# A hybrid encoder layer: an eleventh tile in the long convolution's ring, its room from shared gate rows and from two norm weights folded into the output matrix

## The chip, the cores and the metric

The kernel runs on one core of a Trainium2 chip. The core's engines work side by side, each through its own list of instructions: TensorE (PE) multiplies matrices into the banks of PSUM, VectorE (DVE), ScalarE (ACT) and GpSimd (POOL) do the elementwise work, and SyncE (SP) does nothing but issue transfers between the device memory (DRAM) and the on-chip memory (SBUF, 128 partitions). Transfers are carried by 16 DMA engines. The metric is the device time of one execution in microseconds (us), as a median over several runs.

## What is computed

One layer of a bidirectional encoder over 2048 positions of width 1024, in float32. A projection feeds two mixers: a Hyena group (512 channels), whose long convolutions are done through Fourier transforms, and an mLSTM group (4 heads of 128). Each mixer's output is normalised by groups with a weight per channel, the two are put side by side, and one output matrix follows; then cross-attention to 256 memory rows, and a feed-forward block. The part that matters:

```python
def _group_rms_norm(x, g, n_groups):
    xg = x.reshape(*lead, n_groups, c // n_groups)
    xg = xg * rsqrt(mean(xg * xg, axis=-1, keepdims=True) + EPS)
    return xg.reshape(*lead, c) * g

for o, gate in enumerate((g1, g2)):                       # Hyena
    conv = irfft(rfft(z, n=2 * L) * spec[:, o], n=2 * L)[:, :L]
    z = gate * (conv + z * skip[o])

y_hy = _group_rms_norm(_hyena(...), hy_norm_g, 8)         # 8 groups of 64
y_ml = _group_rms_norm(_mlstm_bidirectional(...), ml_norm_g, 4)
mixed = concatenate([y_hy, y_ml], axis=-1)
h = h + mixed @ w_out
h = h + cross_attention(rms_norm(h), rms_norm(mem), wq, wk, wv, wo)
h = h + square(relu(rms_norm(h) @ ff_w1)) @ ff_w2
out = rms_norm(h)
```

## The kernel before

**Matrix products.** Most products are done in three passes on operands split into a high and a low part (L355, L358, L359). `split` makes the two parts with one copy on ScalarE and one subtraction on VectorE (L366); `split_gain` does the same with a factor per row (L372 and L373). Weights come through SBUF tiles `wn` of 128x512 (the first block of the attention through `we`), loaded by SP and then split into `wh` and `wl`.

**Order of work.** The layer runs as several generators whose steps are woven together, so that PE has work of one stage while another waits. The Hyena stage runs from about 350 us to about 1090 us beside the input projection. The projection of the memory rows for the attention (`memproj`) runs beside the last inverse transform, and the mLSTM scan and the attention come behind it. The instructions of a woven program are then ordered by the framework's scheduler, from its own estimates of when each can start. Each engine runs its list in order. A transfer is issued by an engine's queue, again in order: SP issues nearly all loads, POOL most of the stores, ACT a few. [...]

**The Hyena stage** (the function `hyena`) works on tiles of 128x1024 floats (512 KB), all from one ring with the tag `a`: `ta()` takes the next place in turn, and whoever takes it waits until all readers and writers of the tile that had the place before are done. The ring has ten places. The function's steps:

- Forward transform, 8 steps `j2`: `load1` loads a tile of `hy`, `spectrum` multiplies it (L173 and L186, the two lines of `beside`, which puts eight small products side by side on PE) and stores the result with a transfer of POOL.
- Frequency loop, 16 steps `i` for each of the two orders `o`: `load_filter` loads a block of the filter two steps ahead (`dm` and `fs`, L920), `load2` loads a block of the signal's spectrum one step ahead (`em`, L949, and `zs`), `response` makes the tiles `hr` and `hi`, then comes the complex product on VectorE, ScalarE and POOL, and `back` (L987 to L989) multiplies back and stores `gs` to `zg` with POOL. A step takes five ring places.
- Inverse transform, 8 steps `j2` for each `o`: `load3` loads two tiles of `zg` (L339) and one `gate` tile (L974), one step ahead; `beside` multiplies; VectorE multiplies by the gate (L1051). For `o` = 0 the next spectrum follows. For `o` = 1 the group norm follows, which takes a fourth place: POOL squares (L1060), VectorE sums, `bank_rsqrt` makes the reciprocal root in a PSUM bank, VectorE multiplies by it (L1064), POOL multiplies by the norm weight `ghy` (L1066, two products of 128x512) and issues four stores to `yh` (L1068).

The norm weights `ghy` and `gml` are vectors of 512 numbers, loaded into all 128 partitions by `bcast` (L377, on ACT's queue).

**memproj** multiplies on PE at L708 (keys' and values' weights `wm` with the memory rows `mt`), L725 (with `wq_t`) and L737 (with `wo`); its weights are loaded at L415, a few items ahead.

**The mLSTM scan** multiplies and scans chunk by chunk; for two chunks of 128 rows at a time it normalises: 64 instructions in all at L1356 multiply a head's 128x128 by its reciprocal root, which lies in a PSUM bank, and by `gml`. The bank is one of four that PE's products also use (L1322).

**The attention** takes blocks of 256 columns of `w_out` (16 of them, four for each of four column groups of the sequence), one block ahead, through `columns`.

Of the kernel before, what the change touches and what calls it, by code (L numbers as in the profile page):

```python
# [10 lines left out]
F32 = mybir.dt.float32  # L11
# [3 lines left out]
ALU = mybir.AluOpType  # L15
# [6 lines left out]
CH = 512  # L22
# [78 lines left out]
def packed(given):  # L101
    f32 = np.float32
    par = np.zeros((128, 192), f32)

    def put(at, v):
        v = np.asarray(v, f32).reshape(-1, 128).T
        par[:, at:at + v.shape[1]] = v

    for i, n in enumerate(("norm_mix_g", "norm_mem_g", "norm_x_g", "norm_ff_g")):
        put(8 * i, given[n])  # L110
    for i in range(3):
        put(32 + 20 * i, given["hy_conv_w"][0, i])
        put(44 + 20 * i, given["ml_conv_w"][0, i])
    put(92, given["hy_conv_b"])
    put(104, given["ml_conv_b"])
    par[:, 112:128] = given["ml_gate_b"]
    fw = np.zeros((128, 1280), f32)
    w3 = given["hy_filt_w3"][0].reshape(64, 2, 2, CH)
    for h in range(2):
        own = slice(64 * h, 64 * h + 64)  # L120
        for i, n in enumerate(("b1", "freq1", "b2", "freq2")):
            par[own, 128 + i] = given["hy_filt_" + n][0]
        fw[33 * h:33 * h + 33, own] = given["hy_filt_w1"][0]
        fw[own, 128 + 64 * h:192 + 64 * h] = given["hy_filt_w2"][0]
        fw[own, 256:] = w3[:, :, h].reshape(64, 2 * CH)
    return {"par": par, "fw": fw}


class Prog:
    def __init__(self, ctx, tc, a):  # L130
# [27 lines left out]
        self.cb, self.gb = par[:, 92:112], par[:, 112:128]  # L158
# [46 lines left out]
    def bank_rsqrt(self, pool, ss, n):  # L205
        nc, c = self.nc, ss.shape[1]
        m, ys = (pool.tile([128, c], F32, tag="br" + x, name="br" + x, bufs=2) for x in "my")
# [218 lines left out]
    def inproj_open(self, es):  # L426
# [22 lines left out]
        self.rx, self.rm = small[:, 340:356], small[:, 356:358]  # L449
# [455 lines left out]
    def hyena(self, es):  # L905
# [19 lines left out]
        def ta():  # L925
            return sb.tile([128, 2, CH], F32, tag="a", name="a", bufs=10)
# [5 lines left out]
        e2 = sb.tile([128, 64], F32, name="e2")[:, 0:32]  # L932
        nc.sync.dma_start(out=e2, in_=a["c_e2"])
        ghy = self.bcast(sb, a["hy_norm_g"], CH, "ghy")
# [78 lines left out]
        for o in range(2):  # L1013
# [27 lines left out]
            for j2 in range(8):  # L1041
# [19 lines left out]
                ms = sb.tile([128, 16], F32, tag="ms", name="ms", bufs=2)  # L1061
                nc.vector.tensor_reduce(ms, sqv, AX.X, ALU.add)
                rv = self.bank_rsqrt(sb, ms, 64)
                nc.vector.tensor_tensor(sqv, y, rv.unsqueeze(2).broadcast_to([128, 16, 64]), ALU.mult)  # L1064
                for jj in range(2):
                    nc.gpsimd.tensor_tensor(sq[:, jj], sq[:, jj], ghy, ALU.mult)  # L1066
# [9 lines left out]
    def gates(self):  # L1076
# [4 lines left out]
        with tc.tile_pool(name="m_g", bufs=1) as sg:  # L1081
            gts = sg.tile([128, 16, 16], F32, name="gts")
            nc.sync.dma_start(out=gts, in_=gt.rearrange("(n p) g -> p n g", p=128))
            arr = [sg.tile([128, 2, 16, 4], F32, name=f"arr{i}") for i in range(2)]
# [72 lines left out]
            negM = sg.tile([128, 128], F32, name="negM")  # L1157
            inter = sg.tile([128, 128], F32, name="inter")
# [68 lines left out]
    def mlstm(self, es):  # L1227
# [12 lines left out]
        gml = self.bcast(sb, a["ml_norm_g"], CH, "gml")  # L1240
# [58 lines left out]
        for n in range(16):  # L1299
# [51 lines left out]
            if n % 2:  # L1351
                rv = self.bank_rsqrt(sb, ss, 128)
                for i, y in enumerate(ys):
                    t0 = 128 * (n - 1 + i)
                    for h in range(4):
                        nc.vector.scalar_tensor_tensor(y[:, h], y[:, h], rv[:, 4 * i + h:4 * i + h + 1],  # L1356
                                                       gml[:, 128 * h:128 * h + 128], ALU.mult, ALU.mult)
# [41 lines left out]
    def columns(self, w, stage=None):  # L1399
# [4 lines left out]
        for k0 in range(0, 8 // (3 - n), n):  # L1404
            nat = (stage or self.stage)().rearrange("p (k c) -> p k c", k=n)
            self.nc.sync.dma_start(out=nat, in_=w[:, k0:k0 + n])
            self.split(hi[:, k0:k0 + n], lo[:, k0:k0 + n], nat)
# [31 lines left out]
    def attention(self, es):  # L1439
# [10 lines left out]
        for c in range(4):  # L1450
            items += [a["w_out"][0][:, 256 * i:256 * i + 256].rearrange("(k p) c -> p k c", p=128) for i in range(4)]
            items += [gd[h][:, 4 * k:4 * k + 4] for h in range(2) for k in range(2)] + [vw[i] for i in range(4)]

        def stream():
            nxt = self.columns(items.pop(0), lambda: A.tile([128, 512], F32, tag="e", name="we", bufs=4))
            for w in items:
                cur, nxt = nxt, self.columns(w)
# [750 lines left out]
```

## Time and profile before

| | before |
|---|---|
| median of 3 runs (lowest, highest) | 3053.21 us (3049.87, 3053.69) |
| the profiled execution | 3050.45 us |
| its span, first to last instruction | 3048.7 us |
| busy: PE, DVE, ACT, POOL | 97%, 64%, 49%, 41% |
| mean granted clock of PE | 0.992 |
| moved by DMA | 607 MB, 199 GB/s over the span |

The profile records one execution. A row of the waits reads: engine and line, what it waited for and the line that made that, then microseconds in total, how often, and the longest. A row of the timeline gives the start, the duration, the instruction and, in brackets, the idle time ahead of it and what ended it. A float32 product is recorded in two halves, so the counts in the timeline are twice those of the program. The page in 40 slices, which shows that PE is full nearly everywhere and that transfers crowd in some stretches (the slices are 76 us each):

```profile
PE   9999999998999899999999999999999999999998
...
DMA  6655677686876986474748366658544654444434
```

### The profile page before, as it was taken

How to read it: one execution, taken by the hardware profiler on the slowest of the kernel's cores; microseconds unless marked ns; L12 is line 12 of the kernel's file. 1: busy time of each engine (PE TensorE's matmuls, PEld its weight loads, DVE VectorE, ACT ScalarE, POOL GpSimd, SP SyncE). 2: the span in 40 equal slices, each digit the busy share in tenths (PEclk: the TensorE clock that was granted, in tenths of full speed). 3: DMA queues.
4: the chain of work that ended last, by engine and by line, in shares of the span. 5: the costliest groups of instructions: out<-in, count | busy, mean ns of one | idle time of the engine just before them, and what ended most of it. 6: DMA issues, size and time to landing. Idle time of an engine off the chain costs nothing.

```text
span 3048.7 us, 44157 instructions
## 1 busy us (share of the span) xinstructions
PE 2972.4 (97%) x14799; PEld 2359.1 (77%) x14799; DVE 1943.9 (64%) x3442; ACT 1491.5 (49%) x2930; POOL 1265.0 (41%) x1025
## 2 busy tenths in 40 slices
PE   9999999998999899999999999999999999999998
PEld 7666667775677677888888888887888888888876
DVE  8856464567755557777655665657555686566685
ACT  6443465544664245564544455556555543333335
POOL 0112123321443765152214247765655464345653
PEclk9999999999999999999999999999999999999999
DMA  6655677686876986474748366658544654444434
GB/s 223 191 184 173 210 261 224 198 272 216 277 237 210 324 300 217 140 238 125 236 154 305 116 221 215 203 169 258 180 152 153 213 188 160 130 147 133 143 101 166
DMA packets 423643, 607.03 MB, mean 199 GB/s; under 512 B 36846, under 2 KB 229998, under 8 KB 422392
## 3 DMA queue, kind: packets, MB, share of 16 engines
q1 hardware_dynamic: 395972, 525.42, 53.7%
q0 software_dynamic: 18992, 62.96, 5.6%
q10 hardware_dynamic: 8452, 15.83, 1.4%
q8 instruction: 117, 1.92, 0.3%
q14 instruction: 110, 0.90, 0.1%
HBM read 401.67 MB, written 202.41 MB: 198 GB/s over the span
## 4 chain that ended last, share of the span: by engine, by line
PE 75%; DMA 8%; DVE 6%; issue 6%; ACT 2%; POOL 2%; SPq 1%; DVEq 0%; POOLq 0%; ACTq 0%
PE mm L355 16%; PE mm L359 15%; PE mm L358 15%; PE hy L359 6%; PE hy L355 6%; PE hy L358 6%; PE hy L1030 2%; PE mm L956 2%; PE hy L173 2%; PE hy L987 1%; DMA a<-hy 1%; DMA a<-zg 1%; DVE wl L366 1%; PE hy L1200 1%; PE mm L737 1%
## 5 line engine op out<-in xcount | busy, mean ns | idle before, releaser
L1693 ACT CAST ah<-w 128x512 fp32r<-128x512 f32 x284 | 176.6, 623 | 302.5 <-PE hy L358 155.9
L1694 DVE TENSOR_TENSOR bl<-wr,bh 128x512 fp32r<-128x512 f32 x213 | 237.5, 1119 | 127.1 <-ACT bh L1693 127.0
L366 DVE TENSOR_TENSOR wl<-wn,wh 128x512 fp32r<-128x512 f32 (+1 forms) x296 | 215.5, 771 | 101.7 <-ACT wh L366 101.5
L355 PE MATMUL mm<-xh,wh 128*128 128x512 f32 x640 | 265.5, 416 | 3.9 <-ACT st L201 1.5
L358 PE MATMUL mm<-xl,wh 128*128 128x512 f32 x640 | 256.1, 400 | 4.6 <-DVE xl L366 4.5
L359 PE MATMUL mm<-xh,wl 128*128 128x512 f32 x640 | 253.3, 396 | 0.0
L1693 ACT CAST bh<-wr 128x512 fp32r<-128x512 f32 x232 | 143.5, 620 | 224.2 <-PE mm L359 171.9
L1694 DVE TENSOR_TENSOR al<-w,ah 128x512 fp32r<-128x512 f32 x236 | 217.2, 921 | 56.0 <-ACT ah L1693 55.7
L359 PE MATMUL mm<-bh,al 128*128 128x512 f32 x576 | 224.3, 392 | 4.0 <-DVE al L1694 4.0
L355 PE MATMUL mm<-bh,ah 128*128 128x512 f32 x576 | 226.3, 393 | 0.1
L358 PE MATMUL mm<-bl,ah 128*128 128x512 f32 x576 | 225.4, 391 | 0.0
L366 ACT CAST wh<-wn 128x512 fp32r<-128x512 f32 (+1 forms) x296 | 164.8, 620 | 90.1 <-PE mm L359 34.2
L355 PE MATMUL mm<-act,wh 128*128 128x512 f32 x512 | 198.9, 394 | 2.3 <-ACT wh L366 2.2
L358 PE MATMUL mm<-act,wh 128*128 128x512 f32 x512 | 200.8, 392 | 0.0
L359 PE MATMUL mm<-act,wl 128*128 128x512 f32 x512 | 199.9, 392 | 0.0
L355 PE MATMUL hy<-bh,ah 128*128 128x512 f32 x448 | 175.2, 391 | 0.0
L358 PE MATMUL hy<-bl,ah 128*128 128x512 f32 x448 | 174.6, 390 | 0.0
L359 PE MATMUL hy<-bh,al 128*128 128x512 f32 x448 | 174.4, 390 | 0.0
L331 POOL TENSOR_TENSOR b<-b 128x512 f32<-128x512 f32 x32 | 48.2, 1507 | 294.2 <-DVE b L330 289.8
L355 PEld LDWEIGHTS mm<-xh,wh 128*128 128x128 f32 x640 | 120.9, 189 | 53.5 <-issue 19.7
L358 PEld LDWEIGHTS mm<-xl,wh 128*128 128x128 f32 x640 | 121.2, 189 | 49.9 <-issue 19.4
L355 PE MATMUL mm<-wh,xh 128*128 128x256 f32 (+1 forms) x512 | 155.2, 303 | 1.8 <-DVE a L960 1.8
(396 smaller groups left out, 8240.5 us busy)
## 6 DMA issues: line engine op xcount, KB each, us to landing
wr<-hc SPq DMA_DIRECT2D x224, 256.0 KB
w<-in_ff_w_dram SPq DMA_DIRECT2D x172, 256.0 KB
hc<-wn SPq DMA_DIRECT2D x128, 256.0 KB
wn<-in_w_in_dram SPq DMA_DIRECT2D x100, 256.0 KB
hc<-q SPq DMA_DIRECT2D x96, 256.0 KB
fs<-a SPq DMA_DIRECT2D x32, 512.0 KB
zs<-a POOLq DMA_DIRECT2D x32, 512.0 KB, 5.9
a<-fs SPq DMA_DIRECT2D x64, 256.0 KB
```

What stands on the lines that cost most here:

```text
L173: b = self.nc.tensor.matmul(*products[-1], start=True, stop=True)
L331: nc.gpsimd.tensor_tensor(b, f, b, ALU.subtract)
L355: first = mm(ps, lh, rh, start=start, stop=False)
L358: mm(ps, lh, rl, start=False, stop=False)
L359: self.last = mm(ps, ll, rh, start=False, stop=stop)
L366: both = (self.nc.scalar.copy(hi, src), self.nc.vector.tensor_tensor(lo, src, hi.bitcast(F32), ALU.subtract))
L737: mul(p, t[:, m, ms], o_[:, m, ds], start=m == 0, stop=m == 1)
L956: nc.tensor.matmul(pp, dm[:, m], t[:, m], start=True, stop=True)
L987: nc.tensor.matmul(pg, em[:, m], y, start=True, stop=True)
L1030: nc.tensor.matmul(pp, dm[:, m], t[:, m], start=True, stop=True)
L1693: self.nc.scalar.copy(hi, src)
L1694: eng.tensor_tensor(lo, src, hi.bitcast(F32), ALU.subtract)
```

## The change

The ring of `a` tiles gets an eleventh place (4 KB of each partition). The room comes from several edits: `e2`, a constant table, moves into unused columns of the tile `small` (its load, written where it was, is now issued among the first 25 of SP); `ms` and the two small tiles of `bank_rsqrt` have one buffer instead of two in the Hyena stage; the gate rows `negM` and `inter` take the places of `arr0` and `arr1`; and the broadcast vectors `ghy` and `gml` are gone. Their weights are instead packed into the parameter tile `par`, as one column for each block of 128 rows of `w_out` (`g_out`), and `columns` multiplies the rows of `w_out` by them with `split_gain` while it splits them. So POOL's products at L1066 go, the mLSTM's four products of a head become one product for all heads with a broadcast reciprocal root, and the loop over `w_out` splits 256 columns at a time with a gain where it split 512 without.

```diff
...
     par[:, 112:128] = given["ml_gate_b"]
+    put(132, given["hy_norm_g"])
+    put(136, given["ml_norm_g"])
     fw = np.zeros((128, 1280), f32)
...
         self.cw = par[:, 32:92].rearrange("p (i c) -> p i c", i=3)
-        self.cb, self.gb = par[:, 92:112], par[:, 112:128]
+        self.cb, self.gb, self.g_out = par[:, 92:112], par[:, 112:128], par[:, 132:140]
         self.ps = ctx.enter_context(tc.tile_pool(name="ps", bufs=1, space=PSUM))
...
 
-    def bank_rsqrt(self, pool, ss, n):
+    def bank_rsqrt(self, pool, ss, n, bufs=2):
         nc, c = self.nc, ss.shape[1]
-        m, ys = (pool.tile([128, c], F32, tag="br" + x, name="br" + x, bufs=2) for x in "my")
+        m, ys = (pool.tile([128, c], F32, tag="br" + x, name="br" + x, bufs=bufs) for x in "my")
         nc.scalar.activation(m, ss, AF.Identity, bias=self.eps, scale=1.0 / n)
...
         self.carry = small[:, 0:340].rearrange("p (c t) -> p c t", c=20)
-        self.rx, self.rm = small[:, 340:356], small[:, 356:358]
+        self.rx, self.rm, self.e2 = small[:, 340:356], small[:, 356:358], small[:, 384:416]
         win = a["w_in"][0]
...
         def ta():
-            return sb.tile([128, 2, CH], F32, tag="a", name="a", bufs=10)
+            return sb.tile([128, 2, CH], F32, tag="a", name="a", bufs=11)
 
...
         f1 = self.f1
-        e2 = sb.tile([128, 64], F32, name="e2")[:, 0:32]
+        e2 = self.e2
         nc.sync.dma_start(out=e2, in_=a["c_e2"])
-        ghy = self.bcast(sb, a["hy_norm_g"], CH, "ghy")
         def load1(j2):
...
                 nc.gpsimd.tensor_tensor(sqv, y, y, ALU.mult)
-                ms = sb.tile([128, 16], F32, tag="ms", name="ms", bufs=2)
+                ms = sb.tile([128, 16], F32, tag="ms", name="ms", bufs=1)
                 nc.vector.tensor_reduce(ms, sqv, AX.X, ALU.add)
-                rv = self.bank_rsqrt(sb, ms, 64)
+                rv = self.bank_rsqrt(sb, ms, 64, 1)
                 nc.vector.tensor_tensor(sqv, y, rv.unsqueeze(2).broadcast_to([128, 16, 64]), ALU.mult)
-                for jj in range(2):
-                    nc.gpsimd.tensor_tensor(sq[:, jj], sq[:, jj], ghy, ALU.mult)
                 for q in range(4):
...
             nc.sync.dma_start(out=gts, in_=gt.rearrange("(n p) g -> p n g", p=128))
-            arr = [sg.tile([128, 2, 16, 4], F32, name=f"arr{i}") for i in range(2)]
+            arr = [sg.tile([128, 2, 16, 4], F32, tag=f"arr{i}", name=f"arr{i}") for i in range(2)]
             rw = []
...
             nc.scalar.activation(dec, dec, AF.Exp)
-            negM = sg.tile([128, 128], F32, name="negM")
-            inter = sg.tile([128, 128], F32, name="inter")
+            negM = sg.tile([128, 128], F32, tag="arr0", name="negM")
+            inter = sg.tile([128, 128], F32, tag="arr1", name="inter")
             nc.vector.tensor_scalar(negM, CM, mc[:, 0:1], -1.0, ALU.max, ALU.mult)
...
         GC, EC = cols[:, 0], cols[:, 1]
-        gml = self.bcast(sb, a["ml_norm_g"], CH, "gml")
         masks = []
...
                     t0 = 128 * (n - 1 + i)
-                    for h in range(4):
-                        nc.vector.scalar_tensor_tensor(y[:, h], y[:, h], rv[:, 4 * i + h:4 * i + h + 1],
-                                                       gml[:, 128 * h:128 * h + 128], ALU.mult, ALU.mult)
+                    nc.vector.tensor_tensor(y, y, rv[:, 4 * i:4 * i + 4].unsqueeze(2).broadcast_to([128, 4, 128]), ALU.mult)
                     stores.append(lambda t0=t0, y=y: nc.gpsimd.dma_start(
...
 
-    def columns(self, w, stage=None):
+    def columns(self, w, gain=None, stage=None):
         hi, lo = self.pair(("wh", "wl"))
...
             self.nc.sync.dma_start(out=nat, in_=w[:, k0:k0 + n])
-            self.split(hi[:, k0:k0 + n], lo[:, k0:k0 + n], nat)
+            if gain is None:
+                self.split(hi[:, k0:k0 + n], lo[:, k0:k0 + n], nat)
+                continue
+            for k in range(k0, k0 + n):
+                self.split_gain(hi[:, k], lo[:, k], nat[:, k - k0], gain[:, k:k + 1])
         return hi, lo
...
         for c in range(4):
-            items += [a["w_out"][0][:, 256 * i:256 * i + 256].rearrange("(k p) c -> p k c", p=128) for i in range(4)]
-            items += [gd[h][:, 4 * k:4 * k + 4] for h in range(2) for k in range(2)] + [vw[i] for i in range(4)]
+            items += [(a["w_out"][0][:, 256 * i:256 * i + 256].rearrange("(k p) c -> p k c", p=128), self.g_out)
+                      for i in range(4)]
+            items += [(gd[h][:, 4 * k:4 * k + 4],) for h in range(2) for k in range(2)] + [(vw[i],) for i in range(4)]
 
         def stream():
-            nxt = self.columns(items.pop(0), lambda: A.tile([128, 512], F32, tag="e", name="we", bufs=4))
+            nxt = self.columns(*items.pop(0), lambda: A.tile([128, 512], F32, tag="e", name="we", bufs=4))
             for w in items:
-                cur, nxt = nxt, self.columns(w)
+                cur, nxt = nxt, self.columns(*w)
                 self.peek = nxt
...
               "ml_gate_b", "hy_filt_b1", "hy_filt_freq1", "hy_filt_b2", "hy_filt_freq2", "hy_filt_w1", "hy_filt_w2",
-              "hy_filt_w3", "xa_wq"):
+              "hy_filt_w3", "hy_norm_g", "ml_norm_g", "xa_wq"):
         del given[n]
```

A scheduler orders the instructions, so the change moves others too. On PE the order is the same up to the last inverse transform. The rows below are PE's there, from the last products of j2 = 5 to behind j2 = 7, the last: `hy<-a,e` is the inverse's product with `e2` (in the change `e2` lies in `small`), `mm<-mt,wm` and `mm<-kt,wm` are memproj's. Before:

```order
3872 L186 MATMUL hy<-a,e_2743 32x512 x7
3873 L725 MATMUL mm<-kt,wm 128x256 x4
3874 L708 MATMUL mm<-mt,wm 128x256 x10
3875 L173 MATMUL hy<-a,e_2743 32x512
3876 L186 MATMUL hy<-a,e_2743 32x512 x7
3877 L708 MATMUL mm<-mt,wm 128x256 x6
3878 L725 MATMUL mm<-kt,wm 128x256 x12
3879 L173 MATMUL hy<-a,e_2743 32x512
3880 L186 MATMUL hy<-a,e_2743 32x512 x7
3881 L725 MATMUL mm<-kt,wm 128x256 x4
3882 L708 MATMUL mm<-mt,wm 128x256 x16
3883 L725 MATMUL mm<-kt,wm 128x256 x4
```

And with the change:

```order
3872 L188 MATMUL hy<-a,small 32x512 x7
3873 L727 MATMUL mm<-kt,wm 128x256 x4
3874 L710 MATMUL mm<-mt,wm 128x256 x16
3875 L727 MATMUL mm<-kt,wm 128x256 x4
3876 L175 MATMUL hy<-a,small 32x512
3877 L188 MATMUL hy<-a,small 32x512 x7
3878 L727 MATMUL mm<-kt,wm 128x256 x8
3879 L175 MATMUL hy<-a,small 32x512
3880 L188 MATMUL hy<-a,small 32x512 x7
3881 L727 MATMUL mm<-kt,wm 128x256 x4
3882 L710 MATMUL mm<-mt,wm 128x256 x16
3883 L727 MATMUL mm<-kt,wm 128x256 x9
```

Between j2 = 5 and j2 = 6 stand 24 products of memproj in the place of 14, and between j2 = 6 and j2 = 7 stand 8 in the place of 18. Behind j2 = 7 both have 4 and 16 products before those with the next `wq_t`.

On SP, these are the issues from the loads for j2 = 6 on: `a<-zg` and `a<-hy` are the inverse's loads of two spectrum tiles and of the gate, `wm` the weights of memproj. Before:

```order
388 L415 DMA wm<-in_xa_wq_t_dram 128x1024 x2
389 L339 DMA a<-zg_2739 128x1024 x2
390 L974 DMA a<-hy 32x1024 x4
391 L415 DMA wm<-in_xa_wv_dram 128x4x256 x2
392 L339 DMA a<-zg_2739 128x1024 x2
393 L415 DMA wm<-in_xa_wq_t_dram 128x1024
394 L974 DMA a<-hy 32x1024 x4
395 L415 DMA wm<-in_xa_wq_t_dram 128x1024
396 L415 DMA wm<-in_xa_wv_dram 128x4x256 x2
```

And with the change:

```order
388 L417 DMA wm<-in_xa_wq_t_dram 128x1024 x2
389 L341 DMA a<-zg_2739 128x1024 x2
390 L975 DMA a<-hy 32x1024 x4
391 L417 DMA wm<-in_xa_wv_dram 128x4x256 x2
392 L341 DMA a<-zg_2739 128x1024 x2
393 L975 DMA a<-hy 32x1024 x4
394 L417 DMA wm<-in_xa_wq_t_dram 128x1024 x2
395 L417 DMA wm<-in_xa_wv_dram 128x4x256 x2
```

The load of `wq_t` that stood between the loads of j2 = 7 and their gate stands behind the gate now, in one piece with its second half.

On POOL, these are the first steps of the last inverse: L1060 squares (L1061 in the change), L1066 multiplies by the norm weight, L1068 (L1067) stores `yh`, L896 (L898) stores a piece of the projection. Before:

```order
192 L1060 TENSOR_TENSOR a<-a 128x1024
193 L896 DMA od<-st 128x2x256 x2
194 L1060 TENSOR_TENSOR a<-a 128x1024
195 L1066 TENSOR_TENSOR a<-a,ghy 128x512 x2
196 L896 DMA od<-st 128x2x256
197 L1068 DMA yh<-a 32x1024 x4
198 L1066 TENSOR_TENSOR a<-a,ghy 128x512 x2
199 L1060 TENSOR_TENSOR a<-a 128x1024
```

And with the change:

```order
192 L1061 TENSOR_TENSOR a<-a 128x1024
193 L898 DMA od<-st 128x2x256 x2
194 L1061 TENSOR_TENSOR a<-a 128x1024
195 L1067 DMA yh<-a 32x1024 x4
196 L898 DMA od<-st 128x2x256
197 L1067 DMA yh<-a 32x1024 x4
198 L1061 TENSOR_TENSOR a<-a 128x1024
```

The products are gone; the first two groups of stores both come ahead of the third square, where the second stood behind it.

Over the whole program POOL has 16 instructions fewer, ScalarE 62 more (64 more copies with a gain, two loads less), and VectorE 16 more: 128 products of 128x256 with a gain for 64 of 128x512 without, and 16 products of 128x512 for 64 of 128x128.

## The prediction

> **What bounds the kernel now.** I read the page's first part, then the waits of the matrix engine (PE), then the stretches around the longest of them, then what the sync engine's DMA queue (SPq) waits for there.
>
> ```profile
> PE 2972.4 (97%) x14799; PEld 2359.1 (77%) x14799; DVE 1943.9 (64%) x3442; ACT 1491.5 (49%) x2930; POOL 1265.0 (41%) x1025
> ```
>
> PE is busy 2972.4 of 3048.7 us. The change removes no matmul (13302 in the program before and after) and leaves their order alone up to the last inverse transform, so all that it can win is idle PE time, 3048.7 - 2972.4 = 76.3 us, and what a lowered clock costs after a stall. These are the waits that the change comes near (line, what was waited for: us in total, times, longest):
>
> ```profile
> PE hy L173 <- DMA a<-zg: 8.2, 4, 3.0
> PE mm L725 <- DMA wm<-in_xa_wq_t_dram: 4.7, 1, 4.7
> ...
> PE hy L1030 <- DMA a<-zs: 3.5, 1, 3.5
> ...
> PE hy L1322 <- DVE ht L1356: 1.1, 1, 1.1
> ```
>
> Most are waits for a transfer. Whether the transfer was late because its ring tile was late (what an eleventh tile mends) or because the DMA engines were full (what it does not mend) is the question. The stretches behind three of the stalls, and most of the last inverse, give the busy time of PE, its weight loads, DVE, ACT and POOL (with counts), then the granted clock, the DMA share and GB/s:
>
> ```profile
> 384.00:386.00 2.00, 2.00 (x6) 1.62 (x5) 1.97 (x3) 0.75 (x2) 0.96 (x2) 0.51 1.03 339
> 386.00:388.00 2.00, 2.00 (x7) 1.54 (x7) 1.33 (x2) 0.69 (x1) 0.10 (x1) 0.64 0.98 354
> ...
> 1020.00:1025.00 5.00, 3.62 (x8) 2.53 (x9) 0.40 (x1) 0.00 (x0) 0.00 (x0) 0.50 0.97 312
> ...
> 1055.00:1060.00 5.00, 4.03 (x22) 2.30 (x23) 2.58 (x4) 0.00 (x0) 4.53 (x7) 0.66 1.05 359
> ...
> 1000.00:1100.00 100.00, 91.08 (x497) 74.14 (x497) 51.89 (x150) 29.69 (x82) 73.24 (x83) 0.95 1.01 340
> ```
>
> In each the DMA engines are full. Each stall is followed by a dip of the clock: 2 x (0.49 + 0.36) = 1.7 us lost after the one at 382, 5 x 0.5 = 2.5 us after the one at 1021, 5 x 0.34 = 1.7 us after the one at 1056. What held the DMA queue, in the last inverse (960 to 1080 us):
>
> ```profile
> SPq L415 <- DMA a<-zg: 12.9, 8, 3.4
> ...
> SPq L415 <- PE mm L708: 6.0, 1, 6.0
> SPq L974 <- DMA a<-hy: 5.6, 9, 2.5
> ```
>
> and in the first frequency loop (400 to 640 us):
>
> ```profile
> SPq L949 <- PE hy L987: 74.6, 11, 13.9
> ```
>
> A late ring tile would stand here as a wait for the reader of an `a` tile: for L173, for L1051, for L1066. None of the quoted rows is one. In the last inverse the queue waits for its own earlier transfers to land and for weight tiles (`wm`); in the frequency loop it waits for the two `em` buffers (L949, 74.6 us), which the change leaves at two. **So I take the ring not to be the bound** where PE stalls, and count the eleventh tile itself at nothing but the reordering that it brings.
>
> **The change part by part.** The two broadcast loads go; each is 128 x 512 x 4 bytes = 256 KB. Their rows, and PE's at the stall behind the first:
>
> ```profile
> L377 ACTq DMA_DIRECT2D ghy<-in_hy_norm_g_dram x1: 362/362/362, 355.0 to 355.0; - x1
> L377 ACTq DMA_DIRECT2D gml<-in_ml_norm_g_dram x1: 357/357/357, 1009.3 to 1009.3; - x1
> ```
>
> ```profile
> 382.27 0.61 PE L173 MATMUL hy<-a,f 32*64 32x512 f32 x1 [2.21 <-DMA a<-hy]
> ```
>
> `ghy` starts at 355.0, ahead of the `hy` load for which PE waits 2.21 us at 382; at 350 GB/s its bytes take 0.75 us. With the `e2` load, which moves to the start of the kernel (one issue, 0.36 us by the rows above), that `hy` load lands about 1.1 us earlier. What is left of the stall is half, and so I take half of the dip behind it: -1.1 - 0.8 = **-1.9** (bounds 0, if the queue in front takes the room, and -3.9, stall and dip both).
>
> `gml` starts at 1009.3, just before the weights `wq_t` that PE waits for until 1021.4. Its 256 KB at 312 to 340 GB/s are **-0.8** (bounds 0 and -0.8 with half of the 2.5 us of dip, -2.1).
>
> In the last inverse PE's own order changes. PE's timeline of before, with the waits in brackets:
>
> ```profile
> 1021.38 9.46 PE L725 MATMUL mm<-kt,wm 128*128 128x256 f32 x32 [4.67 <-DMA wm<-in_xa_wq_t_dram]
> ...
> 1045.32 1.99 PE L725 MATMUL mm<-kt,wm 128*128 128x256 f32 x8
> 1048.42 4.55 PE L708 MATMUL mm<-mt,wm 128*128 128x256 f32 x20 [1.10 <-DMA wm<-in_xa_wk_dram]
> 1055.97 0.59 PE L173 MATMUL hy<-a,e 64*32 64x512 f32 x1 [3.00 <-DMA a<-zg]
> ...
> 1057.47 4.02 PE L708 MATMUL mm<-mt,wm 128*128 128x256 f32 x12
> 1061.33 5.34 PE L725 MATMUL mm<-kt,wm 128*128 128x256 f32 x24
> 1066.61 0.60 PE L173 MATMUL hy<-a,e 64*32 64x512 f32 x1
> ```
>
> An issued matmul is two rows here: ten take 4.55 us, so 0.455 us each. Ahead of the seventh tile pair (the one at 1055.97) stood 4 + 10 of them, and now stand 4 + 16 + 4: ten more, 4.55 us, over a wait of 3.0. That wait goes, with its 1.7 us of clock. But ahead of the eighth pair only 8 stand where 18 stood. PE then asks for the eighth at 1045.3 + 1.1 + 24 x 0.455 + 1.5 + 8 x 0.455 = 1062.5. When it can be there, SPq tells:
>
> ```profile
> 1044.63 0.85 SPq L339 DMA_DIRECT2D a<-zg  x2
> 1045.99 3.93 SPq L974 DMA_DIRECT2D a<-hy  x4
> 1050.90 1.60 SPq L415 DMA_DIRECT2D wm<-in_xa_wv_dram  x2
> 1053.96 2.28 SPq L339 DMA_DIRECT2D a<-zg  x2
> ```
>
> The seventh pair's load took from 1044.63 to 1055.97, 11.3 us; the eighth was issued at 1053.96, and would by that be there at 1065.3; by its own and the waiting 1 MB of `wv` alone (2 MB at 359 GB/s, 5.8 us after 1056.2) at 1062. So the wait comes back at 0 to 2.8 us. Of the 4.7 us won I keep about half: **-2.5** (bounds 0 and -4.7). That `wq_t` is now issued behind the eighth pair's load and gate speaks for the lower landing time, and costs nothing at its own consumer, which stands 20 matmuls (9 us) later.
>
> The arithmetic of the gains:
>
> ```profile
> L1066 POOL TENSOR_TENSOR a<-a,ghy 128x512 f32<-128x512 f32 x16 | 20.1, 1277 | 4.8 <-DVE a L1064 3.2 <-DMA a<-hy 1.3
> ...
> L1356 DVE SCALAR_TENSOR_TENSOR ht<-ht,hy,gml 128x128 f32<-128x128 f32 x64 | 20.0, 382 | 0.7
> ```
>
> POOL loses 20.1 us of multiplies between 992 and 1084. Nobody on PE waits for them; behind them on POOL are the `yh` stores, which go out 2 x 1.28 = 2.6 us earlier. Those are 4 x 128 KB = 512 KB, and the second and third of them now meet the `wq_t` load at 1012: between 0 and 512 KB / 340 GB/s = 1.5 us of delay for it, and as much again at 1048. I take **+1.5** (bounds 0 and +3).
>
> [...]
>
> VectorE's 64 products of 128x128 (382 ns) become 16 of 128x512, whose nearest row is another 128x512 product with a bank:
>
> ```profile
> L1294 DVE TENSOR_TENSOR rw<-rw,hy 128x512 f32<-128x512 f32 x32 | 20.4, 679 | 6.5 <-PE hy L1284 3.9 <-ACT rw L1293 2.6
> ```
>
> 16 x 0.68 = 10.9 us for 20.0. The bank that PE waits 1.1 us for (L1322 behind L1356) comes free two tiles' worth earlier, 2 x (4 x 0.382 - 0.68) = 1.7 us: **-0.9** (bounds 0 and -1.1).
>
> The gain is now put on the 16 blocks of 256 columns of `w_out`, per block eight half-width pairs in the place of four full ones:
>
> ```profile
> L366 DVE TENSOR_TENSOR wl<-wn,wh 128x512 fp32r<-128x512 f32 x288 | 210.2, 772 | 95.9 <-ACT wh L366 95.7
> L366 ACT CAST wh<-wn 128x512 fp32r<-128x512 f32 x288 | 160.2, 619 | 89.2 <-PE mm L359 34.2 <-PE mm L358 29.9 <-DMA wn<-vw 11.9
> ...
> L689 DVE SCALAR_TENSOR_TENSOR mt<-xt,par,rb x8: 477/480/485, 985.3 to 988.2; 128x256 f32<-128x256 f32 x8
> ...
> L372 ACT ACTIVATE act<-acc,par 128x512 fp32r<-128x512 f32 x32 | 22.8, 712 | 8.6 <-DVE acc L1517 8.3
> ...
> L1194 ACT ACTIVATE ve<-va,cols 128x129 f32<-128x129 f32 x60 | 19.2, 391 | 21.3 <-DMA va<-vd 20.1 <-DVE cf L1202 0.9 <-PE hy L1200 0.3
> ...
> 1200.00:1400.00 200.00, 198.19 (x1089) 169.82 (x1087) 156.58 (x404) 117.77 (x345) 77.53 (x63) 1.00 0.56 182
> ```
>
> ScalarE with a gain takes 391 ns at 129 columns and 712 at 512, so about 0.48 at 256: 8 x 0.48 - 4 x 0.619 = +1.4 us a block, 22 us in all. VectorE: 8 x 0.480 - 4 x 0.772 = +0.75, 12 us. In 1200 to 1400 PE is busy 99% while ACT is 59% and VectorE 78%, and blocks are split one ahead, so I cost it at **0**; if that cover were gone, a block would cost PE up to 1.4 us, and PE would show it as waits for `wh` or `wl`. The buffers of `ms`, `brm` and `bry` (two to one) and the shared gate rows make VectorE and ScalarE wait for readers some 10 us back: 0.
>
> **Sum**, against the profiled execution: 3050.45 - 1.9 - 0.8 - 2.5 + 1.5 - 0.9 = 3045.85, that is 4.6 us less. That execution lies 2.8 us under the median of the three runs, 3053.21, and the changed kernel will be timed as a median too: 3053.2 - 4.6 = **3048.6**. Best bounds together: -3.9 - 2.1 - 4.7 - 1.1 = -11.8. About 0.2%, 6 us, is what a measurement of this kernel can tell from no change.
>
> **The rivals.**
> A (forecast, 0.48): the small terms as summed, 3046 to 3052.
> B (0.24): the freed bytes and the new order are enough to end all of these stalls, and the dips with them: 11.8 us, 3041.4. For it: the stalls at 382 and 1056 are short, 2.2 and 3.0 us, so that a microsecond or two less may spare the whole dip. Against: the DMA share of 1.01 over 1000 to 1100, from which only 256 KB go.
> [...]
> C (0.16): it does not do what it says. More room changes no landing, because the queue waits for its own transfers; the stall at 1056 reappears at the eighth pair, the one at 382 is filled by the transfers behind it. 0 to -1 us, 3052 to 3053.5.
> D (0.12), the other side: with ten tiles and five taken in a step, each kind of tile falls on its own place of two steps before; with eleven the places rotate, and the load of a filter block (two steps ahead) gets the place of a spectrum tile three steps back, so that SPq now waits for a store on POOL's queue to land. The stores of that kind, in 445 to 470:
>
> ```profile
> L989 POOL DMA_DIRECT2D zg<-a x4: 556/556/556, 450.7 to 468.0; - x4
> ...
> DMA to landing us min/median/max: 3.9/5.2/7.1
> ```
>
> Their landing, at most 7.1 us, is well inside the slack of about a step (some 11 us and more), so it should cost nothing. It decides where POOL is that late, as when it is held behind other work, and then every load behind it on SPq is late too, those of weights included. Its price in one step is a stall like the one of 3.5 us at L1030; four of the 32 steps would be 14, less the 4.6: +9.4, 3062.6.
>
> **How the numbers follow.** Range 3041 to 3056: it reaches to B's end below, and above takes in C and the part of D with two steps; D's upper part is left out. Faster by over 0.2% is under 3047.1: B and a quarter of A, 0.36. Slower by over 0.2% is over 3059.3: most of D, 0.11. Between: 0.53.
>
> **What would show it.** In the changed profile the wait of L175 for `hy` at 382 should be near 1 us, the one for the seventh `zg` pair gone and one for the eighth in its place, the wait for `wq_t` near 4 us, and L1322's gone. ACT should be some 20 us busier, POOL 20 us less. Wrong would be waits of PE for `wh` or `wl` of `w_out`, waits of SPq L922 (the filter's load) for `zg`, or stalls in the frequency loops that were not there.

## The result, and the profile after

The changed kernel is slower: 3057.59 us as a median of 15 runs (3054.02 to 3063.89), beside 3050.05 us (3044.45 to 3057.60, 15 runs) of the kernel before on the same chip. The ratio is 1.0024, with a 95% interval of 1.0016 to 1.0032. The forecast was 4.6 us less, in a range up to 3056; the measured change is some 7.4 us more. The profiled execution took 3059.25 us, its span 3057.5.

The page's first part shows where not to look. PE is as busy as before, ScalarE has 17.6 us more, VectorE 7.0 more and POOL 21.5 less:

```profile
PE 2974.2 (97%) x14799; PEld 2358.9 (77%) x14799; DVE 1950.9 (64%) x3458; ACT 1509.1 (49%) x2994; POOL 1243.5 (41%) x1009
```

The longer waits of PE that answer to those quoted of before, and the new ones (the same line's number differs by one or two between the kernels):

```profile
PE hy L175 <- DMA a<-zg: 13.8, 4, 6.7
PE hy L1199 <- ACT ht L1334: 6.9, 2, 5.2
...
PE hy L1320 <- DVE rw L1292: 3.6, 2, 2.1
PE hy L1031 <- DMA a<-zs: 3.5, 1, 3.5
...
PE mm L357 <- ACT act L368: 2.3, 1, 2.3
...
PE mm L727 <- DMA wm<-in_xa_wq_t_dram: 2.1, 2, 1.1
```

The wait for `hy` (2.2 us) is gone, the one for `wq_t` has shrunk from 4.7 to 2.1, but the one for `zg` has grown from 8.2 to 13.8, and three are new. The longest of them is L1199, a product of the mLSTM scan, behind ScalarE's work on `ht`; the others are L1320 behind VectorE's `rw` (3.6 us, none before) and a wait for `act` (2.3 us). PE's timeline where two of them stand:

```profile
1051.74 0.59 PE L175 MATMUL hy<-a,small 64*32 64x512 f32 x1 [1.65 <-DMA a<-zg]
...
1063.16 1.03 PE L175 MATMUL hy<-a,small 64*32 64x512 f32 x1 [6.68 <-DMA a<-zg]
...
1127.50 2.08 PE L1199 MATMUL hy<-ve,kn 128*128 128x129 f32 x8 [5.15 <-ACT ht L1334]
```

And the busy time of PE (first of the five engine columns) from the scan to the end of the attention, of the kernel before and then of the change:

```profile
1080.00:1700.00 620.00, 614.11 (x3132) 510.54 (x3131) 418.93 (x992) 330.52 (x891) 232.67 (x192) 1.00 0.63 209
```

```profile
1080.00:1700.00 620.00, 605.79 (x3086) 502.67 (x3085) 416.11 (x993) 339.78 (x943) 219.09 (x182) 0.99 0.62 204
```

PE stands idle 620 - 614.1 = 5.9 us there before, and 14.2 us in the change. That is a stretch in which the prediction had put nothing but one gain of 0.9 us. ScalarE's own waits in it name what it stood in front of:

```profile
ACT ht L1334 <- DMA ym<-ht: 20.7, 4, 9.1
```

In the kernel before:

```profile
ACT ht L1336 <- DMA ym<-ht: 3.5, 1, 3.5
```

ScalarE writes the scan's next `ht` tile (L1334). There are two such tiles, and it has to wait until the store of the tile's former content to `ym` has landed; everything behind it in ScalarE's list waits too. L1199 on PE is released by L1334 itself. The likely reason is the PSUM bank: L1334 reads one under the name `hy`, and L1199 writes one.

```profile
1126.82 1.14 ACT L1334 ACTIVATE ht<-hy,den 128x128 f32<-128x128 f32 x4 [9.07 <-DMA ym<-ht]
```

Such a row counts the whole idle time, whatever else would have held the instruction. L1334 also needs `den` from VectorE, which was ready at 1120.65, and the store landed at 1126.74. So 6.1 of the 9.07 us belong to the store alone. In all four waits together it is 10.7 of the 20.7 us, and next to nothing of the 3.5 us of the kernel before.

### The profile page after: what moved, and what is told of

Same layout as the page of the kernel before. It is cut to its first block, busy times and chain, and to the rows that moved or that the text cites. A ratio compares the mean times of both kernels' runs of the same rounds, so it can differ in the third digit from the quotient of the medians.

```text
span 3057.5 us, 44231 instructions
## 1 busy us (share of the span) xinstructions
PE 2974.2 (97%) x14799; PEld 2358.9 (77%) x14799; DVE 1950.9 (64%) x3458; ACT 1509.1 (49%) x2994; POOL 1243.5 (41%) x1009
## 4 chain that ended last, share of the span: by engine, by line
PE 76%; DMA 7%; DVE 7%; issue 4%; ACT 3%; POOL 2%; SPq 1%; ACTq 0%; DVEq 0%; POOLq 0%
PE mm L357 16%; PE mm L360 16%; PE mm L361 16%; PE hy L357 6%; PE hy L361 6%; PE hy L360 6%; PE hy L175 2%; PE mm L957 2%; PE hy L1031 2%; PE hy L988 1%; DMA a<-zg 1%; DMA hy<-st 1%; DMA ym<-ht 1%; POOL ssum L1524 1%; DVE wl L375 1%
## 5 line engine op out<-in xcount | busy, mean ns | idle before, releaser
L368 DVE TENSOR_TENSOR wl<-wn,wh 128x512 fp32r<-128x512 f32 (+1 forms) x236 | 168.4, 760 | 92.6 <-ACT wh L368 92.6
L368 ACT CAST wh<-wn 128x512 fp32r<-128x512 f32 (+1 forms) x236 | 130.2, 621 | 74.2 <-PE mm L361 42.5
```

The lines of the kernel that those rows point to most:

```text
L368: both = (self.nc.scalar.copy(hi, src), self.nc.vector.tensor_tensor(lo, src, hi.bitcast(F32), ALU.subtract))
```

## The experiments

All ratios are to runs of the kernel before on the same chip, from five rounds, with 95% intervals; 0.001 is 3.05 us.

**The parts of the change.** Four kernels, to tell the ring, the splitting and the two folded weights apart.

`ring10`, the changed kernel with `bufs=10`:

> The changed kernel with ten ring tiles in the place of eleven; all else as changed, and the order of the instructions is the same on every engine. Theory 1 (the loss comes from the new order of the last inverse and the scan, not from the ring): about 1.0024 of the kernel before, like the change, with a stall of some 6 to 7 us at the eighth tile pair and one of 5 us at L1199. Theory 2 (the splitting of w_out with a gain): the same 1.0024. Theory 3 (rotating places make SP wait for stores): back to 1.000 or below. If the eleventh tile had brought the gains ahead of 1000 us, this run would lose them and be slower than the change, near 1.005.

Measured 1.0014 (1.0005 to 1.0023), with a wait of 6.64 us at the eighth pair and, at L1199, one of 2.1. The early gains are there without the eleventh tile. Against the change, 1.0024, the difference is within the uncertainty.

`no_gain`, the changed kernel with

```diff
-            items += [(a["w_out"][0][:, 256 * i:256 * i + 256].rearrange("(k p) c -> p k c", p=128), self.g_out)
+            items += [(a["w_out"][0][:, 256 * i:256 * i + 256].rearrange("(k p) c -> p k c", p=128), None)
```

> The changed kernel without the gain on w_out: its blocks are split 512 wide as before, and the two norm weights are left out of the result. Theory 1: as the change, 1.002 to 1.003, with the same stall of 6 to 7 us at the eighth pair. Theory 2: ScalarE loses some 20 us of work and the kernel comes back to 1.000 or below, 0.998 if the early gains stay.

Measured 0.9984 (0.9975 to 0.9993): 0.4%, 12 us, less than the change. Its order on PE is that of the change up to the scan, and the stall at the eighth pair is there in full:

```profile
1066.63 1.03 PE L175 MATMUL hy<-a,small 64*32 64x512 f32 x1 [7.28 <-DMA a<-zg]
...
1080.00:1700.00 620.00, 616.38 (x3154) 513.29 (x3153) 404.45 (x946) 330.23 (x891) 228.40 (x186) 1.00 0.63 208
```

Idle from 1080 to 1700 us: 3.6 us. So the stall at the eighth pair, the largest in the profile of the change, does not decide. Theory 2 stands, and the order of the last inverse is not the loss here. The order of the scan differs as well (on PE from 1109 us on), so that part of theory 1 is still open.

`no_ghy`, the kernel before without the load of `ghy` and POOL's products at L1066:

> The kernel before without the Hyena group's norm weight: its load and POOL's 16 products are left out, all else as before. Its order on PE between the seventh and eighth tile pair is that of the change (24 and 8 products of memproj). Theory 1: the stall at the eighth pair appears here too, 5 to 7 us, and the result is between 1.000 and 1.003. Theories 2 and 3: no such stall from this edit, the early gain of 2 to 5 us stays, 0.998 to 0.9995.

Measured 1.0010 (1.0000 to 1.0020), with the stall of 6.46 us at the eighth pair, as theory 1 had it: a new order costs time here without any new splitting. Behind the `ht` of this kernel, too, PE has a wait of 2.4 us (1129.47), and ScalarE's longest for a store to `ym` is 7.6 us. `no_gain`, with the same order of the last inverse, is 0.26% faster; which of its other edits does that is not told apart. The early gain is there too, and was larger than I had put it; PE's rows at the start of the forward transform and behind its end, of before and of `no_ghy`:

```profile
351.67 0.64 PE L173 MATMUL hy<-z,f 32*64 32x512 f32 x1 [1.10 <-ACT a L311]
...
419.96 0.50 PE L355 MATMUL mm<-xh,wh 128*128 128x512 f32 x1 [0.38 <-DVE st L203]
```

```profile
350.79 0.64 PE L173 MATMUL hy<-z,f 32*64 32x512 f32 x1 [1.10 <-ACT a L311]
...
415.04 0.50 PE L355 MATMUL mm<-xh,wh 128*128 128x512 f32 x1 [0.38 <-DVE st L203]
```

68.3 us between them, and 64.3. Of the kernels profiled here the others that load both vectors also show 68.0 to 68.4, and all eight that do not load `ghy` 64.2 to 64.5: the stall of 2.2 us and the whole dip of 1.7 behind it are gone. The five that load `ghy` alone show 65.5 to 66.5; they have a stall of 1.0 to 2.0 us there and a clock of 1.00 behind it. Further on less of this is left: the first pair of the last inverse starts at 974.3 us in the mean of the eight, at 975.5 in that of the other nine, and each group spreads over 4 to 7 us.

`no_gml`, the kernel before without the load of `gml`, and with the one product per head group of the change:

```diff
-        gml = self.bcast(sb, a["ml_norm_g"], CH, "gml")
...
-                    for h in range(4):
-                        nc.vector.scalar_tensor_tensor(y[:, h], y[:, h], rv[:, 4 * i + h:4 * i + h + 1],
-                                                       gml[:, 128 * h:128 * h + 128], ALU.mult, ALU.mult)
+                    nc.vector.tensor_tensor(y, y, rv[:, 4 * i:4 * i + 4].unsqueeze(2).broadcast_to([128, 4, 128]), ALU.mult)
```

> The kernel before without the mLSTM group's norm weight: its load is left out, and four products of a head become one with the broadcast reciprocal root. Its order has 15 products of memproj between the seventh and the eighth tile pair, and 21 ahead of the seventh. Theory 1: the stall at the eighth pair is smaller than in the change by the 7 products more, 3.2 us (3 to 4 us left in the place of 6.7), and the result near 1.000. Theories 2 and 3: 0.999 to 1.000 for the 256 KB and the earlier bank.

Measured 0.9976 (0.9966 to 0.9986), better than any of the theories had it. Its eighth pair waits 0.7 us, and for VectorE's bank, not for `zg`. From the first pair to the eighth it takes 88.7 us, beside 91.8 before; the five kernels with this order take 88.7 to 90.7, the four with the order of before 91.8 to 94.5. With the 2 us at the start that is the greater part of its 7 us.

**The splitting by itself.** The four kernels differ in order as well, so the next ones add the splitting alone to kernels whose order up to the attention it leaves as it is.

`split_ones`: the kernel before with the new `columns`, a gain of 1.0 for all rows, both weights where they were.

> The kernel before with the new splitting of w_out alone: 256 columns at a time with a gain, and the gain is 1.0 (both norm weights stay where they were). The order on PE up to the attention is that of the kernel before. Theory A (the splitting costs the time, as no_gain against the change says: 0.4%): 1.003 to 1.004 of the kernel before, with new waits of PE for the splits or for ScalarE between 1100 and 1250 us, and none at the eighth tile pair. Theory B (the new order of the last inverse and the scan costs it, and no_gain was faster because it lost that order's later part): 1.000 to 1.001.

Measured 1.0010 (1.0001 to 1.0019): the upper end of theory B, and theory A is out for this kernel. From 1080 to 1700 us PE is idle 6.1 us, beside 5.9 before. So in this order the splitting costs little.

`ml_full`: `no_gml` with its weight folded into `w_out` by the new splitting.

> The kernel before with the mLSTM's norm weight folded into the rows of w_out by the new splitting (all eight blocks of rows; the Hyena group's factor there is 1.0 and its own multiply stays). Against no_gml this adds only the splitting. Theory A: no_gml's 0.9976 plus 0.3 to 0.4%, so 1.0006 to 1.0016. Theory B: 0.9976 to 0.9985.

Measured 1.0002 (0.9992 to 1.0011), between the two theories, and 0.26% above `no_gml`. From 1080 to 1700 us PE is idle 10.6 us here and 5.7 there.

`ml_half`: as `ml_full`, with the four blocks of the Hyena group's rows split 512 wide.

```diff
-            if gain is None:
+            if gain is None or k0 not in (4, 6):
```

> As ml_full, but only the four blocks of rows that belong to the mLSTM are split with the gain 256 wide; the other four 512 wide as before. Theory A: half of the splitting's cost, 0.9976 plus 0.2%: 0.999 to 1.000. Theory B: 0.9976 to 0.9985, as ml_full.

Measured 0.9987 (0.9978 to 0.9997), about halfway between `no_gml` and `ml_full`, and between the two theories.

`ml_pool`: the kernel before with the one product per head group, and behind it

```diff
+                    nc.gpsimd.tensor_tensor(y, y, gml.rearrange("t (h e) -> t h e", h=4), ALU.mult)
```

> The kernel before with the mLSTM's four products of a head as one with the broadcast reciprocal root, and the norm weight multiplied by POOL behind it (32 products of 128x512 of some 1.28 us less or more, nothing folded). The order on PE in the last inverse is that of the kernel before, and the load of the weight stays. If the one product in the place of four is what made no_gml faster (the bank free sooner): 0.998 to 0.999. If it was the order of the last inverse (15 products between the last two pairs, no stall there): 1.000, with the stalls of the kernel before.

Measured 0.9998 (0.9989 to 1.0007), as the second of the two has it: the order of the last inverse. The single product did not make this kernel faster; how much POOL's product, which now stands in front of the store, takes back is not told apart.

**ScalarE's wait for `ht`.** The price of the splitting differs by kernel: 0.10% on the kernel before, 0.26% on `no_gml`, 0.40% on `no_gain`. In the last of these ScalarE's wait for the store to `ym` goes with it: 4.0 us in `no_gain`, 20.7 in the change, 17.1 in `ring10`. The row of `no_gain` misses one wait, which the profile puts down to VectorE:

```profile
1124.10 1.14 ACT L1334 ACTIVATE ht<-hy,den 128x128 f32<-128x128 f32 x4 [5.21 <-DVE rw L1273]
```

L1334 does not read `rw`; `den` was ready at 1121.46, and the store landed at 1124.01. Counted as the time that the store alone costs ScalarE, `no_gain` has 3.8 us, the change 10.7 and `ring10` 6.9. PE does not wait there: in `no_gain` six rows of memproj (L739, from 1122.71 to 1125.29) stand directly in front of the scan's L1199, and in the change they stand further ahead (at 1116.97). On the kernel before the wait stays at 3.2 us with the splitting, and in `ml_full` (8.8) it is what it is in `no_gml` (8.9). A third tile takes the wait away and leaves the splitting's work.

`third_ht`, the changed kernel with

```diff
-                    y = sb.tile([128, 4, 128], F32, tag="h0", name="ht", bufs=2)
+                    y = sb.tile([128, 4, 128], F32, tag="h0", name="ht", bufs=3)
```

> The changed kernel with three buffers in the place of two for the scan's tile ht, which in the change ScalarE waits for until its store to ym has landed (20.7 us in four waits, the longest 9.1; 3.5 us in the kernel before, 4.0 in no_gain). Theory A1 (the splitting costs time by way of that wait: the scan's steps fall so that ScalarE stands in front of a tile whose store is under way, and PE behind it): these waits go, PE's 5.2 and 1.8 us at L1199 too, and the result is 0.999 to 1.0005 of the kernel before, 6 to 10 us less than the change. Theory A2 (it costs time by ScalarE's and VectorE's longer work itself): 1.0015 to 1.0025, as the change.

Measured 0.9987 (0.9978 to 0.9996): 0.37%, 11 us, less than the change. ScalarE has no wait for `ym` left. The instruction that waited 9.07 us, and PE's stretch:

```profile
1121.51 1.14 ACT L1334 ACTIVATE ht<-hy,den 128x128 f32<-128x128 f32 x4 [3.10 <-DVE den L1329]
...
1080.00:1700.00 620.00, 613.96 (x3140) 510.53 (x3139) 425.73 (x1007) 346.20 (x954) 222.18 (x185) 1.00 0.63 207
```

ScalarE and VectorE do all the work of the splitting here (346.2 and 425.7 us in the stretch, more than in the change), and PE is idle 6.0 us in the place of 14.2. At 1064.19 PE waits 6.63 us for the eighth pair, as in the change. Up to 1346 us of the change the instructions stand in the same order as in the change, so up to there nothing but the third tile differs. The product that waited at L1199 starts at 1122.84 in the place of 1127.50, and what starts at 1340.10 in the change starts at 1331.62 here, 8.5 us earlier. Behind that some hundred of PE's rows stand elsewhere, and the rest of the gain comes with them.

`third_ht_half` (`ml_half` with the third tile):

> ml_half (only the mLSTM's weight folded, ten ring tiles) with the third buffer. Theory A1: little is left to win, since ScalarE waited 4.5 us there and PE not for it; 0.998 to 0.9985. Theory A2: 0.9985 to 0.999, as ml_half.

Measured 0.9976 (0.9966 to 0.9987): the fastest of the kernels with the full result, and faster than both theories had it.

`third_ht_before` (the kernel before with the third tile):

> The kernel before with the third buffer alone. Both theories: 0.9995 to 1.000, as PE has no wait behind that store there; if it is faster by more than 0.1%, the third buffer is worth something by itself, and third_ht must be read against this.

Measured 1.0000 (0.9989 to 1.0010): the third tile by itself shows no gain, to within 0.1%.

`gain_on_pool`, the changed kernel with POOL multiplying each piece by the gain and the splits 512 wide:

> The changed kernel with the gain multiplied into each piece of w_out by POOL (64 products of 128x512, 1.3 us each) and the splitting on ScalarE and VectorE 512 wide as before. Theory A2 (ScalarE's and VectorE's work): back to no_gain's 0.9984 or a little above, if POOL (41% busy) is not late. Theory A1: between, since the order of the scan changes again; it is read by ScalarE's waits for ht.

Measured 1.0036 (1.0020 to 1.0051), a miss for both. ScalarE's wait for `ym` is 20.7 us again, and from 1080 to 1700 us it now waits 22.2 us for POOL's pieces of `w_out` as well. It moves work off ScalarE and is slower than the change; it says nothing clean about either theory.

**What was still open.** Three kernels with the third tile, in which the late stalls no longer cover the rest.

`third_ht_ring10` (`bufs=10` for the ring):

> third_ht with ten ring tiles; the order of the instructions is the same on every engine. If the ring is worth nothing either way (the waits of SP in the profile of before): 0.998 to 0.9995, the 0.9987 of third_ht within its uncertainty. If the eleventh tile brought the early gains: above 0.9995. If it costs by the rotating places (the rival D): below 0.998.

Measured 0.9995 (0.9985 to 1.0005), beside 0.9987 with eleven. The other pair, 1.0014 with ten and 1.0024 with eleven, points the other way by as much. No effect of the eleventh tile can be told, in either direction. Read the other way, the two pairs price the third `ht` tile: 0.37% (11 us) with eleven ring tiles and 0.19% (6 us) with ten, each to within some 0.13%.

`third_ht_18_14`: `third_ht` with one matmul, and so those behind it in its group, tied behind the seventh pair's last product:

```diff
+                    if self.nproj == 3 and 8 * m + k == 10:
+                        self.tc.add_manual_dep(d.ins, self.sixth.ins.name, mybir.DependencyInfo(
+                            mybir.DependencyClass.NoSync, mybir.DependencyReason.DATA), reason="behind")
```

> third_ht with the last six products of one memproj group held behind the seventh tile pair, so that 18 and 14 products stand ahead of the seventh and the eighth in the place of 24 and 8 (what stands behind the eighth pair shifts a little too). If the wait of 6.6 us at the eighth pair is a plain lack of work there: it falls by 6 x 0.455 = 2.7 us to some 4, the seventh's wait grows by as much or less, and the time is the same or up to 2.5 us less, 0.998 to 0.999. If the new order were the loss: 3 us or more less, below 0.998.

Measured 0.9986 (0.9977 to 0.9995), the same as `third_ht`. The wait at the eighth pair fell from 6.6 to 2.6 us and the seventh's rose from 1.0 to 2.2:

```profile
1055.95 0.59 PE L175 MATMUL hy<-a,small 64*32 64x512 f32 x1 [2.15 <-DMA a<-zg]
...
1065.88 0.59 PE L175 MATMUL hy<-a,small 64*32 64x512 f32 x1 [2.60 <-DVE hy L217]
```

`third_ht_full` (`ml_full` with the third tile):

> ml_full (the mLSTM's weight folded with the new splitting of all rows, the Hyena group's own multiply kept, ten ring tiles) with the third ht buffer. If the splitting costs only by way of ht's two buffers: 0.9975 to 0.998, as no_gml (0.9976) and third_ht_half (0.9976). If it has a price of its own beside that: 0.9985 or more.

Measured 0.9992 (0.9983 to 1.0002): 0.10% less than `ml_full`, but 0.16% more than `no_gml`. So a part of the splitting's price in that order, up to some 5 us, does not come by way of `ht`; on `third_ht` against `no_gain` it is 0.03%, 1 us. The traces point to VectorE: at L1323 (L1320 in the change) PE waits for it 6.0 us in `ml_full`, 4.1 in `third_ht_full` and 1.1 in `no_gml`. No run tries that.

## Why the prediction was wrong, by its own steps

**The step that failed** is the one on `w_out`: "so I cost it at 0". Its sizes were near for ScalarE (0.498 us for a half, estimated 0.48) and low for VectorE (0.625 in the mean, estimated 0.480):

```profile
L375 DVE SCALAR_TENSOR_TENSOR wl<-wn,par,wh 128x256 fp32r<-128x256 f32 x120 | 69.0, 625 | 19.6 <-ACT wh L374 19.4
L374 ACT ACTIVATE wh<-wn,par 128x256 fp32r<-128x256 f32 x120 | 51.3, 498 | 15.1 <-DMA wn<-in_w_out_dram 9.8 <-PE mm L360 5.1
```

But the cover named for it was the wrong one. I asked whether the splits would be ready for PE, found ScalarE 59% busy and PE 99%, and named waits for `wh` or `wl` as the sign of a mistake. PE waits 2.1 us for `wh` in the change and 3.3 in the kernel before. What grew is the wait of another consumer on ScalarE's list: the scan, woven into the same stretch, whose next tile hung on a store. With the splitting the scan's steps and the store fell so that ScalarE reached L1334 up to 9 us before the landing. It is not the splits' own time that stands in front of the longest wait: ScalarE splits the first block of `w_out` from 1097 to 1103 us and the next from 1162 us on. What the splitting changed there is, as far as the traces show, the order. The change against `no_gain` prices all this at 12 us, and `third_ht` recovers 11 with all splits in place (6 with ten ring tiles). Nor did the prediction follow the order beyond the last inverse, where the splitting shifts some four hundred of PE's rows against `no_gain`.

**The other terms.** Without the splitting the sum holds: `no_gain` is 0.9984, 4.9 us less, where the prediction had -4.6. That is a sum of errors that cancel, as far as the profiles tell:

- `ghy` and `e2`, -1.9: the stall and its dip both went, 4.0 us, the bound of -3.9, though only some 1 us of it is left in the mean at the start of the last inverse. The granted clock behind the place was 0.51 before and is now full:

```profile
384.00:386.00 2.00, 2.00 (x10) 1.43 (x8) 1.85 (x3) 0.14 (x1) 1.06 (x2) 1.00 0.97 293
```

- The new order of the last inverse, -2.5: no gain. The wait at the eighth pair was put at 0 to 2.8 us and is 6.5 to 7.3 in five of the seven kernels with 24 and 8 products, and between 4.5 and 6.2 in the other two. The clock fell behind it as it had behind the seventh's (0.66 there):

```profile
1063.00:1065.00 2.00, 1.84 (x16) 0.26 (x16) 0.00 (x0) 0.00 (x0) 0.00 (x0) 0.50 1.01 327
1065.00:1070.00 5.00, 5.00 (x21) 4.00 (x14) 3.14 (x7) 1.17 (x2) 1.41 (x3) 0.55 0.82 285
```

  The error is in the landing: the eighth pair's load was issued at 1049.4, and PE could go on at 1063.2, 13.8 us later; I had allowed 8 to 11.3. The load also went out 12.1 us behind the sixth pair's start, where it was 9.7 before. From the first pair to the eighth the change takes 92.3 us, the kernel before 91.8 (90.1 to 96.0 over the seven kernels with this order), and `third_ht_18_14` took the six products back at no difference in time. Of what the early part had won, 3.9 us at the first pair (970.86 in the place of 974.80), most goes in the dip behind the eighth: the scan's next product, L1282, starts at 1079.86 with five more products done (2.3 us), L1284 before at 1078.10, so 0.5 us is left there. `no_gain` pays this too and is still faster than the kernel before; the rest of the loss, some 8 us of idle PE, comes after 1080.
- `gml`, -0.8, and the earlier stores, +1.5: not told apart. The wait for `wq_t` is between 1.9 and 6.7 us in the profiles with no clear link to either.
- The bank, -0.9: L1320 waits 0.2 us for `ht` in the place of 1.1, as forecast. `ml_pool`, at 0.9998, shows no gain beyond that, to within 0.09%, 3 us. The same product's new waits for `rw`, 3.6 us, were not foreseen.

**The rivals.** B fell with the eighth pair's stall; its argument that a shorter stall spares the whole dip holds at 382 us, where the clock is 1.00 behind stalls of 1.0 to 2.0 us and 0.50 or 0.51 behind 2.0 to 2.4 us. C was right on the ring, as far as can be told, and on the stall that reappears at the eighth pair, and wrong on the one at 382, which went. (That SP's queue waits for its own transfers holds: the 1944 transfers of SP and ACT in the kernel before use eight completion semaphores, 243 on each, and in 1898 of 1936 cases all 16 signals of a transfer were in when the next one on its semaphore went out.) D, the slower one, had the sign but not the place: SPq's waits for a store of `zg` in 400 to 640 us are 4.3 us (4.2 before), its filter load (L922) has no wait for `zg`, and 9.7 us of waits for stores to `zs` over the whole kernel, where it had 7.6, and no difference between ten tiles and eleven can be told.

## What to carry to other kernels

Folding a factor into a streamed weight turns one multiply into a multiply for every pass over that weight, here 64 wide splits into 128 narrow ones. Before it is costed at nothing because its consumer is covered, every other user of the two engines in the same stretch has to be looked at, above all those that stand in line in front of a buffer whose store is still under way: the spare time of an engine's average says nothing about them. The scheduler's new order has to be read there too, since the wait that a change moves need not stand next to the instructions that it adds. When a change adds work there, a further buffer for the tile that it waits for (2 KB of each partition here, no gain before the change) is the first thing to try.

## What was not expected of the hardware

The first four stores of 256 KB to `ym` landed 2.9 to 4.6 us after their issue in the kernel before and 5.3 to 9.1 us in the change, with the DMA engines 0.77 to 0.97 busy meanwhile in the one and 0.72 to 0.91 in the other; over all 16 it is 2.2 to 4.8 and 2.3 to 9.1 us. A load of 1 MB of `wo` weights was issued 6 us ahead of the first such store before, and 0.5 us ahead in the change (1117.16 and 1117.61). That load is not reason enough: in `ring10` and `third_ht` it goes out 0.6 us ahead of the store, and the store lands in 5.9 and 5.6 us. Why it took 9.1 us in the profile of the change stays open.

A stall of 2.2 us that goes took its whole clock dip with it: 4.0 us in all, in each of the eight kernels that did not load `ghy`, though only 1.1 us of earlier data were counted for it. In the kernel before the clock fell to 0.51 behind that stall, from 384 to 386 us. At that place the four kernels with stalls of 2.0 to 2.4 us fell to 0.50 or 0.51, and the five with 1.0 to 2.0 us stayed at 1.00. The length alone does not decide: behind the stall of 2.5 us at 644 us the kernel before stayed at 1.00 as well.
